# The up product of an MLP as seven block products for groups two to four, with sums of the rows beside group one

## The chip, the core and the metric

The kernel runs on one core of a Trainium2 chip. The core has TensorE (PE in the profile) for matrix products, VectorE (DVE) and ScalarE (ACT) for element-wise work, GpSimd (POOL) and SyncE (SP), which here mainly issue transfers, and 16 DMA engines that the issued transfers share. A product accumulates in a bank of PSUM of 128 x 512 numbers. The metric is the device time of one execution, in microseconds; shorter is better.

## The reference

A layer of 512 tokens with 1024 features: a projection, two recurrent branches, a gated mix and its output projection, and then an MLP of 4096 features. All of it is in float32. The change touches the MLP, and the transfers that are made earlier on its behalf:

```python
    mix = (jax.nn.sigmoid(gate_a) * ya + jax.nn.sigmoid(gate_b) * yb) @ w_out
    x = x + rmsnorm(mix, n_mix_post)
    hn = rmsnorm(x, n_mlp_pre)
    ff = jnp.square(jax.nn.relu(hn @ w_up)) @ w_down
    return x + rmsnorm(ff, n_mlp_post)
```

## The kernel before

**Products of split numbers.** A float32 operand is held as a high part, rounded to the shorter float32r, and a low part, the rest. Every product is three matmuls: high by high, high by low, low by high (the helper `mm3`, L93 to L95; L317 in the block products). A weight tile of 128 x 1024 comes as `raw` by a load on SP's queue (L103 from the weights, L197 from block sums); ACT rounds it to `whi` (L148) and DVE subtracts to get `wlo` (L149). There are two `raw` buffers per pool and three of `whi` and `wlo`. One such tile feeds 24 matmuls of 512 columns.

**The MLP.** The 4096 features are done in four groups of 1024. A group is an up product, the squared relu, and a down product that adds into `facc`, four row tiles of 128 tokens. In the up product the features are the output's partitions and the 512 tokens its columns: 64 products of 128 x 128 weights by 512 tokens, 192 matmuls. Group one alone begins while the rows of the residual stream are still being normalised: `mix_done` adds a row tile's norm to `x2`, scales the row (`fw`, L1763), and PE transposes it to `hn` (L397), whose cast is on ACT (L428) and whose low part is on DVE (L429). So group one's first four output tiles take the second 256 tokens first and the first 256 after them, as matmuls of 256 columns.

**Seven products for eight.** The down product of a group is a block product of a 2 x 2 scheme by quarters: rows by a feature half and a token half, weights by a feature half and a column half. Seven products of quarter sums replace eight of quarters: "11", "12", "22" take plain quarters of the rows, "s1" to "s4" take sums. Row sums are made on DVE in `first_sums` (L1828 to L1830) and `other_sums` (L1838), and each is split (L1786: cast on ACT, subtraction on DVE). Weight sums are made by transfers alone (`BlockSums`): a copy of a quarter to DRAM on SP's queue (L169), then an accumulating add on POOL's queue (L135), both of 512 KB. The products of a sum write two banks, `dl` or `mm`, and DVE adds them to `facc` (L1851).

**When the block sums are made.** The copies and adds wait in two lists. `pace` is called at each weight load; when the modelled PE time has passed `queued[0]`, it issues one job behind that load and moves `queued[0]` on by `JOB_US` (8.5), and over the stretch `REST` (860 to 985) in one step. A job that is late is not made up except by one at each following load; a sum that is wanted and not made is made on the spot.

**Order.** A scheduler orders each engine's instructions by data, buffers and priority; after that, each engine runs its own list strictly in order. `high_priority` moves instructions ahead: the weight splits and the first sums are so marked. The two finished row tiles of tokens 0 to 255 (`early`) are stored from `x2` to the output by SP in group three, and the MLP's result is later added to them in DRAM.

## Time and profile before

Three executions took 1328.65, 1331.12 and 1333.48 us, median 1331.12. The execution that was profiled spans 1329.4 us, 1.7 below that median.

| | of the profiled execution |
|---|---|
| span | 1329.4 us |
| PE busy | 1314.3 us, 99% |
| DVE busy | 938.0 us, 71% |
| ACT busy | 663.9 us, 50% |
| POOL busy | 89.6 us, 7% |
| moved by DMA | 223.16 MB, mean 168 GB/s |
| groups two to four, up | 43.52 us each |
| groups two to four, down | 38.08 us each |

A row of instructions gives line, engine, operation, output and inputs by the program's names, shape, count, then the busy time and the mean of one. A row of a window gives the stretch, its length, and each engine's busy time with its instructions, then the clock that PE was granted (1.00 is full speed), the busy share of the DMA engines and the GB/s that they moved. A row of a timeline gives an instruction's start, its duration and, in brackets, the idle time ahead of it with what ended it. Instructions overlap at their ends, so a start-to-start distance is shorter than a duration.

### The profile page before, as it was taken

The page shows a single profiled execution, that of the slowest core. Times are in us where ns is not written, and L with a number is a line of the kernel's source. Part 1 is how long each engine was busy: PE and PEld are TensorE (multiplying, and loading weights), DVE is VectorE, ACT ScalarE, POOL GpSimd, SP SyncE. Part 2 cuts the span into 40 slices and gives each one's busy share as a digit, 9 for nine tenths or more (in the row PEclk, how much of TensorE's full clock was granted, in tenths as well). Part 3 has the DMA queues.
Part 4 walks back from the last instruction along what each step waited for, and adds up shares of the span by engine and source line. Part 5 has one row for each costly group of instructions (what it writes and reads, how often), then busy time and mean ns, then how long its engine had stood idle before and what let it go on. Part 6 is the DMA issues. An engine that isn't in the chain of part 4 may idle for free.

```text
span 1329.4 us, 17531 instructions
## 1 busy us (share of the span) xinstructions
PE 1314.3 (99%) x6591; PEld 1093.6 (82%) x6591; DVE 938.0 (71%) x1569; ACT 663.9 (50%) x1159; POOL 89.6 (7%) x95
## 2 busy tenths in 40 slices
PE   9999999999999999999999999999999999999997
PEld 7888888888788888888888888888889888888886
DVE  6889867586656577877577766889675746738378
ACT  5784335555524533554453353455356636355364
POOL 2201100000010000000010000000001000000001
PEclk9999999999999999999999999999999999999999
DMA  6336944467765665986393472445629896868635
GB/s 191 133 112 159 203 101 94 110 164 194 188 159 151 143 187 142 270 244 155 95 259 89 104 229 80 141 150 173 233 78 248 225 275 147 234 187 225 188 118 135
DMA packets 115558, 223.16 MB, mean 168 GB/s; under 512 B 6983, under 2 KB 38897, under 8 KB 114961
## 3 DMA queue, kind: packets, MB, share of 16 engines
q1 hardware_dynamic: 96496, 175.13, 41.2%
q0 software_dynamic: 16944, 40.54, 18.9%
q10 hardware_dynamic: 2032, 6.36, 1.3%
q8 instruction: 52, 0.85, 0.2%
q14 instruction: 34, 0.27, 0.1%
HBM read 216.75 MB, written 72.37 MB: 217 GB/s over the span
## 4 chain that ended last, share of the span: by engine, by line
PE 89%; DVE 4%; ACT 4%; DMA 2%; issue 1%; DVEq 0%; ACTq 0%
PE mm L668 18%; PE mm L317 16%; PE dl L317 11%; PE mm L95 10%; PE mm L93 10%; PE mm L94 10%; PE dl L668 6%; DMA raw<-sums 1%; PE dl L93 1%; PE tr L397 1%; PE dl L95 1%; PE dl L94 1%; PE tr L677 1%; DVE wlo L149 1%; PE mm L632 1%
## 5 line engine op out<-in xcount | busy, mean ns | idle before, releaser
L149 DVE TENSOR_TENSOR wlo<-raw,whi 128x1024 fp32r<-128x1024 f32 x269 | 328.5, 1223 | 215.7 <-ACT whi L148 214.3
L148 ACT CAST whi<-raw 128x1024 fp32r<-128x1024 f32 x269 | 282.7, 1052 | 376.4 <-PE mm L668 74.6
L668 PE MATMUL mm<-actT,whi 128*128 128x512 f32 x448 | 144.8, 404 | 0.0
L317 PE MATMUL mm<-whi,xsum 128*128 128x512 f32 x384 | 120.6, 390 | 0.0
L95 PE MATMUL mm<-hn,wlo 128*128 128x512 f32 (+1 forms) x288 | 105.4, 366 | 0.0
L94 PE MATMUL mm<-hn,whi 128*128 128x512 f32 (+1 forms) x288 | 105.3, 366 | 0.0
L93 PE MATMUL mm<-hn,whi 128*128 128x512 f32 (+1 forms) x288 | 105.3, 366 | 0.0
L668 PEld LDWEIGHTS mm<-actT,whi 128*128 128x128 f32 x448 | 81.7, 190 | 15.3
L668 PE MATMUL mm<-actT,wlo 128*128 128x512 f32 x224 | 88.4, 395 | 0.0
L317 PEld LDWEIGHTS mm<-whi,xsum 128*128 128x128 f32 x384 | 71.8, 188 | 14.9
L317 PE MATMUL mm<-wlo,xsum 128*128 128x512 f32 x192 | 74.8, 390 | 0.0
L317 PE MATMUL dl<-whi,ffq 128*128 128x512 f32 x224 | 71.2, 389 | 0.0
L668 PE MATMUL mm<-whi,og 128*128 128x512 f32 x192 | 62.4, 397 | 0.0
L95 PEld LDWEIGHTS mm<-hn,wlo 128*128 128x128 f32 x288 | 54.3, 189 | 8.8
L94 PEld LDWEIGHTS mm<-hn,whi 128*128 128x128 f32 x288 | 54.3, 189 | 8.8
L93 PEld LDWEIGHTS mm<-hn,whi 128*128 128x128 f32 x288 | 54.3, 189 | 8.6
L668 PE MATMUL mm<-whi,actT 128*128 128x512 f32 x176 | 60.3, 405 | 1.0 <-DVE qf L906 1.0
L317 PE MATMUL dl<-whi,actT 128*128 128x512 f32 x192 | 61.2, 390 | 0.0
L317 PE MATMUL mm<-whi,ffq 128*128 128x512 f32 x192 | 60.9, 389 | 0.0
L1786 DVE TENSOR_TENSOR ffq<-r,ffq 128x512 fp32r<-128x512 f32 (+1 forms) x64 | 39.2, 622 | 27.8 <-ACT ffq L1786 27.6
L135 POOL DMA_DIRECT2D sums<-in_w_in_dram x28 | 32.6, 1164 | 364.3 <-DMA sums<-in_w_in_dram 364.3
L93 PE MATMUL mm<-actT,whi 128*128 128x512 f32 x128 | 51.5, 402 | 0.0
(391 smaller groups left out, 2843.0 us busy)
## 6 DMA issues: line engine op xcount, KB each, us to landing
raw<-in_w_in_dram SPq DMA_DIRECT2D x95, 512.0 KB, 4.6
raw<-sums SPq DMA_DIRECT2D x64, 512.0 KB, 4.5
raw<-in_w_up_dram SPq DMA_DIRECT2D x36, 512.0 KB, 7.1
sums<-in_w_in_dram SPq DMA_DIRECT2D x32, 512.0 KB, 5.6
sums<-in_w_down_dram SPq DMA_DIRECT2D x32, 512.0 KB, 7.4
sums<-in_w_in_dram POOLq DMA_DIRECT2D x28, 512.0 KB, 7.5
raw<-in_w_down_dram SPq DMA_DIRECT2D x24, 512.0 KB, 4.2
sums<-sums POOLq DMA_DIRECT2D x20, 512.0 KB, 8.4
```

Of the source, the lines that this page charges most:

```text
L93: nc.tensor.matmul(ps, lh, rh, start=first, stop=False)
L94: nc.tensor.matmul(ps, lh, rl, start=False, stop=False)
L95: nc.tensor.matmul(ps, ll, rh, start=False, stop=last)
L135: tc.keep_in_program_order(nc.gpsimd.dma_start(dst, src, accum_op=ALU.add))
L148: nc.scalar.copy(hi[:, :n], raw[:, :n])
L149: nc.vector.tensor_tensor(lo[:, :n], raw[:, :n], hi[:, :n], ALU.subtract)
L317: m = nc.tensor.matmul(pss[t], lhs[i // 2], rhs[i % 2], start=first and k + i == 0, stop=k + i == 5, skip_group_check=not first,)
L397: nc.tensor.transpose(ps, src, ident)
L632: pin(nc.tensor.matmul(first_keys[f][:, 256:512], ws[w][:, kk, :], xs[x][:, 2 * j + kk, 256:512], start=False, stop=kk == 1 and i == 2, sk ...
L668: m = tc.keep_in_program_order(nc.tensor.matmul(*args, **kwargs))
L677: tc.keep_in_program_order(nc.tensor.transpose(ps, src, ident if by is None else by))
L1786: return nc.scalar.copy(dst[0], r), nc.vector.tensor_tensor(dst[1], r, dst[0], ALU.subtract)
```

## The change

The up product of groups two to four becomes a block product of the same seven-product scheme (`seven_up`). Its row operand is quarters of `hn` and four sums of quarters; its weight operand is quarters of `w_up` and four block sums of them for each of the three groups, which doubles the lists of transfers for the MLP's last three groups: 24 copies and 24 adds more. Each of the seven products is 48 matmuls of 256 columns: 336 matmuls for 192 of 512. It takes 14 weight splits for 8. The seven results are combined by `combine` on DVE, and `Squares.square` applies the squared relu to a whole quarter (forms of 128 x 1024 where there were 128 x 512).

`hidden_sums` makes the four row sums: eight additions or subtractions of 128 x 1024 on DVE, then four casts on ACT and four low parts on DVE. They are written behind group one in the code. Their scratch is `facc`, which moves to the place that `x2` had; `x2` gets tiles of its own, and one of these is the place of a sum once the early rows are stored, a store that moves from SP in group three to POOL ahead of the sums.

`JOB_US` becomes 4.6, except between 480 and 640, where it stays 8.5. In `seven_down` the product "12" stands later in the order of groups two to four: in groups two and three behind "s2" and "s1", in group four still directly behind "11".

```diff
-JOBS_FROM, JOB_US = 70.0, 8.5
+JOBS_FROM, JOB_US, BUSY_JOB_US = 70.0, 4.6, 8.5
+BUSY = 480.0, 640.0
...
-        queued[0] += JOB_US
+        queued[0] += BUSY_JOB_US if BUSY[0] < queued[0] < BUSY[1] else JOB_US
...
-    down_sums = [BlockSums(w_down[grp * D : (grp + 1) * D, :], 0, 512, f"dn{grp}") for grp in range(4)]
-    for sums in [z_sums, ga_sums] + vg_sums + [gb_sums] + down_sums:
+    down_sums, up_sums = [], {}
+    for grp in range(4):
+        if grp:
+            up_sums[grp] = BlockSums(w_up, grp * D, grp * D + 512, f"up{grp}")
+        down_sums.append(BlockSums(w_down[grp * D : (grp + 1) * D, :], 0, 512, f"dn{grp}"))
+    mlp_sums = [sums for grp in range(4) for sums in (up_sums.get(grp), down_sums[grp]) if sums]
+    for sums in [z_sums, ga_sums] + vg_sums + [gb_sums] + mlp_sums:
...
-        x2 = acc.rearrange("p k t -> p (k t)").rearrange("p (t d) -> p t d", t=4)
+        x2 = Rows2([pm.tile([P, 2, D], F32, tag=f"x2{i}", name="x2") for i in range(2)])
...
+            def square(self, th, ch, src):
+
+                r = self.quarter(th, ch)
+                for i in range(2):
+                    nc.scalar.activation(r[:, 2 * i : 2 * i + 2, :], src[i], AF.Relu)
+                nc.scalar.activation(r, r, AF.Square)
+                name = {(0, 0): "11", (0, 1): "12", (1, 1): "22"}.get((th, ch))
+                if name:
+                    split(r, self.dst[name])
+
+            def first_sums(self, f, n=2):
+
+                fs = slice(f, f + n)
                 r11, r21, r22 = self.r[:, 0, 0, fs, :], self.r[:, 0, 1, fs, :], self.r[:, 1, 1, fs, :]
                 nc.vector.tensor_tensor(r22, r21, r22, ALU.subtract)
                 nc.vector.tensor_tensor(r21, r11, r21, ALU.subtract)
                 nc.vector.tensor_tensor(r11, r22, r11, ALU.subtract)
-                self.sums_mark = split(r11, self.fs("s2", f))[0]
-
-            def other_sums(self, f, last):
-
-                r, fs = self.r[:, :, :, f : f + 2, :], lambda name: self.fs(name, f)
+                self.sums_mark = split(r11, self.fs("s2", f, n))[0]
...
-            b = bank(psm)
-            plain(b, "12", 1, 0, True)
-            add(0, 0, b, prio=0)
+            def late():
+                b = bank(psm)
+                plain(b, "12", 1, 0, True)
+                add(0, 0, b, prio=0)
+
+            if not grp:
+                late()
             c = bank(psm)
 
             def s1():
...
                 summed(a, "s3", 3, False)
                 add(1, 1, a, ALU.subtract)
 
-            for step in (s1, s2) if grp == 3 else (s2, s1, s3):
+            for step in (late, s1, s2) if grp == 3 else (s2, s1, late, s3) if grp else (s2, s1, s3):
...
-        facc = pm.tile([P, 4, D], F32, tag="facc", name="facc")
+        facc = cp.tile([P, 4, D], F32, tag="acc", name="facc")
+        hq = {"11": quarter(hn, 0, 0), "12": quarter(hn, 1, 0), "22": quarter(hn, 1, 1)}
+
+        def hidden_sums():
+
+            for t in early:
+                nc.gpsimd.dma_start(out[0, t * P : (t + 1) * P, :], x2[:, t, :])
+
+            def by_features(w):
+                return w.rearrange("p (k t) -> p k t", k=4)
+
+            def pair(name):
+                return [by_features(pm.tile([P, D], F32R, tag="ym", name=name, bufs=4)) for _ in range(2)]
+
+            s1 = pm.tile([P, 2, 4, 256], F32R, tag="x20", name="hsum")
+            places = {
+                0: [s1[:, i] for i in range(2)],
+                1: pair("hsum"),
+                2: pair("hsum"),
+                3: quarter(hn, 0, 1),
+            }
+            a22, a11 = by_features(facc[:, 0, :]), by_features(facc[:, 1, :])
+            a21 = by_features(facc[:, 2, :])
+            a12 = by_features(facc[:, 3, :])
+            sum_quarters(hn, ((a22, a11), a21, a12), lambda i: places[i], hq)
+
+        def seven_up(grp, sq):
+
+            src, c1, sums = w_up, grp * D, up_sums[grp]
+            pinned = []
+
+            def product(pss, x, ks, wts, first):
+                wh, wl = wts
+                xh, xl = hq[x]
+                for f in range(4):
+                    for kk in range(2):
+                        k = 2 * ks + kk
+                        w = [v[:, kk, f * P : (f + 1) * P] for v in (wh, wl)]
+                        tick(768)
+                        for i in range(3):
+                            m = nc.tensor.matmul(
+                                pss[f // 2][:, f % 2 * 256 : f % 2 * 256 + 256], w[i // 2], (xh, xl)[i % 2][:, k, :],
+                                start=first and f % 2 + k + i == 0, stop=k + i == 5, skip_group_check=True,
+                            )
+                            if pinned:
+                                tc.keep_in_program_order(m)
+                            pinned.append(m)
+
+            plain, summed = block_products(src, sums, product)
+
+            def halves_of(th, ch):
+                q = sq.quarter(th, ch).rearrange("p f t -> p (f t)")
+                return [q[:, 512 * i : 512 * i + 512] for i in range(2)]
+
+            def take(th, ch, parts):
+                sq.square(th, ch, [p.rearrange("p (f t) -> p f t", f=2) for p in parts])
+
+            def combine(dst, ps, other, op):
+                with tc.high_priority(400):
+                    for i in range(2):
+                        nc.vector.tensor_tensor(dst[i], ps[i], other[i], op)
+
+            p1, u2 = halves_of(1, 0), halves_of(0, 1)
+            a = bank(psx)
+            plain(a, "11", 0, c1, True)
+            with tc.high_priority(400):
+                for i in range(2):
+                    nc.scalar.copy(p1[i], a[i])
+            b = bank(psm)
+            summed(b, "s2", 2, True)
+            combine(u2, b, p1, ALU.add)
+            plain(a, "12", 1, c1, False)
+            take(0, 0, a)
+            summed(b, "s3", 3, False)
+            combine(p1, b, p1, ALU.add)
+            c = bank(psm)
+            summed(c, "s1", 1, True)
+            combine(halves_of(1, 1), c, p1, ALU.subtract)
+            take(1, 1, halves_of(1, 1))
+            d = bank(psx)
+            summed(d, "22", 4, True)
+            with tc.high_priority(150):
+                combine(p1, d, p1, ALU.add)
+                take(1, 0, p1)
+                sq.first_sums(0, 4)
+            plain(c, "s4", 1, c1 + 512, False)
+            combine(u2, c, u2, ALU.subtract)
+            take(0, 1, u2)
+            sq.other_sums(0, grp == 3, 4)
+
         for grp in range(4):
             sq = Squares(grp)
-            for th in (None,) if grp else (1, 0):
-                tt = slice(0, T) if th is None else slice(256 * th, 256 * th + 256)
+            if grp:
+                seven_up(grp, sq)
+                seven_down(grp, sq.dst)
+                continue
+            for th in (1, 0):
+                tt = slice(256 * th, 256 * th + 256)
                 pss = feature_major(w_up, [h[:, :, tt] for h in hn], grp * 1024, 512, 8)
                 for f in range(4):
                     sq.take(0, f, pss[f], th)
...
                     for i in range(2):
                         sq.take(1, f + i, pss[i])
                     sq.first_sums(f)
-                sq.other_sums(f, grp == 3)
-            if grp == 2:
-                for t in early:
-                    with tc.issue_after(sq.sums_mark.ins):
-                        nc.sync.dma_start(out[0, t * P : (t + 1) * P, :], x2[:, t, :])
+                sq.other_sums(f, False)
+            hidden_sums()
             seven_down(grp, sq.dst)
```

The lines of the changed kernel are shifted by a few: its L104 is L103 before, L136 is L135, L150 is L149, L170 is L169, L198 is L197, L435 is L429, L1745 is L1738, L1770 is L1763, L1793 is L1786, L1848 to L1850 are L1828 to L1830, L1858 is L1838, L1871 is L1851. L223 to L231 are `sum_quarters`, L1976 the store of the early rows, L2030 `combine`.

**First place: DVE in group one, from the second-to-last row tile's norm to the last row's transposes** (`acc` or `x` is the residual row, `hn` here the low part of the transposed row). Before:

```order
L416 SCALAR_TENSOR_TENSOR nr_y<-nr_t,nr_y 128x1
L1738 SCALAR_TENSOR_TENSOR acc<-fw,nr_y,acc 128x512
L429 TENSOR_TENSOR hn<-tr,hn 128x4x128
L149 TENSOR_TENSOR wlo<-raw,whi 128x1024
L429 TENSOR_TENSOR hn<-tr,hn 128x4x128
L1738 SCALAR_TENSOR_TENSOR acc<-fw,nr_y,acc 128x512
L1723 TENSOR_SCALAR nh_v<-nh_s 128x1
L149 TENSOR_TENSOR wlo<-raw,whi 128x1024
```

and, a few rows on:

```order
L1763 SCALAR_TENSOR_TENSOR fw<-acc,nr_y,wmlp 128x512 x2
L149 TENSOR_TENSOR wlo<-raw,whi 128x1024
L429 TENSOR_TENSOR hn<-tr,hn 128x4x128 x2
L149 TENSOR_TENSOR wlo<-raw,whi 128x1024 x4
L1786 TENSOR_TENSOR ffq<-r_8593,ffq 128x256 x2
```

Now:

```order
L1730 TENSOR_SCALAR nh_v<-nh_s 128x1
L223 TENSOR_TENSOR facc<-hn 128x1024
L421 TENSOR_TENSOR nr_t<-nr_t,nh_v 128x1
L1731 SCALAR_TENSOR_TENSOR nh_v<-nh_s,nh_v 128x1
L224 TENSOR_TENSOR facc<-facc 128x1024
L150 TENSOR_TENSOR wlo<-raw,whi 128x1024
L422 SCALAR_TENSOR_TENSOR nr_y<-nr_t,nr_y 128x1
L418 RECIPROCAL nr_y<-nr_y 128x1
L1770 SCALAR_TENSOR_TENSOR fw<-x_8205,nr_y,wmlp 128x512 x2
L150 TENSOR_TENSOR wlo<-raw,whi 128x1024
L435 TENSOR_TENSOR hn<-tr,hn 128x4x128 x2
```

and, at the last row:

```order
L422 SCALAR_TENSOR_TENSOR nr_y<-nr_t,nr_y 128x1
L1770 SCALAR_TENSOR_TENSOR fw<-x_8205,nr_y,wmlp 128x512 x2
L231 TENSOR_TENSOR hsum<-facc,hsum 128x1024
L435 TENSOR_TENSOR hn<-tr,hn 128x4x128 x2
L223 TENSOR_TENSOR facc<-hn 128x1024 x2
L225 TENSOR_TENSOR facc<-facc 128x1024
```

From the end of the third row's norm to the last row's `fw`, three sums of 128 x 1024 (another L223 stands eight rows ahead of the first of these) are now in DVE's list, and seven weight splits instead of five; between that `fw` and the low part of `hn` stands the low part of a row sum. On PE, 205 matmuls of group one's up product stand behind the last row's transposes before, 192 now.

**Second place: DVE where group four's up product hands over to its down product** (`r` is the squared rows, `ffq` the low part of a row operand, `dl` and `mm` banks of PSUM). Before:

```order
L1786 TENSOR_TENSOR ffq<-r_10500,ffq 128x2x256
L149 TENSOR_TENSOR wlo<-raw,whi 128x1024
L1786 TENSOR_TENSOR ffq<-r_10500,ffq 128x2x256
L1828 TENSOR_TENSOR r_10500<-r_10500 128x512
L149 TENSOR_TENSOR wlo<-raw,whi 128x1024
L1829 TENSOR_TENSOR r_10500<-r_10500 128x512
L1851 TENSOR_TENSOR facc<-facc,dl 128x512
L1830 TENSOR_TENSOR r_10500<-r_10500 128x512
```

Now:

```order
L2030 TENSOR_TENSOR r_10923<-dl,r_10923 128x512 x2
L1793 TENSOR_TENSOR ffq<-r_10923,ffq 128x1024
L150 TENSOR_TENSOR wlo<-raw,whi 128x1024
L1848 TENSOR_TENSOR r_10923<-r_10923 128x1024
L150 TENSOR_TENSOR wlo<-raw,whi 128x1024
L2030 TENSOR_TENSOR r_10923<-mm,r_10923 128x512 x2
L1849 TENSOR_TENSOR r_10923<-r_10923 128x1024
L150 TENSOR_TENSOR wlo<-raw,whi 128x1024
L1850 TENSOR_TENSOR r_10923<-r_10923 128x1024
L150 TENSOR_TENSOR wlo<-raw,whi 128x1024
L1871 TENSOR_TENSOR facc<-facc,dl 128x512
L1793 TENSOR_TENSOR ffq<-r_10923,ffq 128x1024
```

followed by `L150`, the second `L1871`, and then two `L1793`, the first of which is the low part of "12". Where two 128 x 512 sums stood between splits, whole quarters now stand: the rows of the first sums are 128 x 1024, and the last quarter's `combine` waits for the last up product. In groups two and three the list reads the same as far as the second `L1871`, except that what is wanted there first is the low part of "s2", the `L1793` ahead of that `L150`.

**Third place: SP's queue at the output projection** (`w_br_b`, `w_out`, `w_up` are loads of weights, `sums<-` are copies for the block sums). Before:

```order
L197 DMA raw<-in_w_in_dram 128x2x512 x2
L103 DMA raw<-in_w_br_b_dram 128x1024 x4
L103 DMA raw<-in_w_out_dram 128x1024 x8
L103 DMA raw<-in_w_up_dram 128x2x512 x4
L1964 DMA out_dram<-acc 128x1024
L103 DMA raw<-in_w_up_dram 128x2x512 x4
```

Now:

```order
L104 DMA raw<-in_w_br_b_dram 128x1024 x2
L170 DMA sums<-in_w_up_dram 128x2x512
L104 DMA raw<-in_w_br_b_dram 128x1024 x2
L170 DMA sums<-in_w_up_dram 128x2x512
L104 DMA raw<-in_w_out_dram 128x1024 x2
L170 DMA sums<-in_w_up_dram 128x2x512
L104 DMA raw<-in_w_out_dram 128x1024 x2
L170 DMA sums<-in_w_up_dram 128x2x512
L104 DMA raw<-in_w_out_dram 128x1024 x2
L170 DMA sums<-in_w_down_dram 128x2x512
L104 DMA raw<-in_w_out_dram 128x1024 x2
L170 DMA sums<-in_w_down_dram 128x2x512
```

Where no job stood among the last loads ahead of the MLP, a copy now stands behind every second one.

21 lines of the change are left out of this document (12 added, 9 removed).

## The prediction

> **What bounds the kernel now.** I began with the page: busy times and the chain of waits.
>
> ```profile
> span 1329.4 us, 17531 instructions
> PE 1314.3 (99%) x6591; PEld 1093.6 (82%) x6591; DVE 938.0 (71%) x1569; ACT 663.9 (50%) x1159; POOL 89.6 (7%) x95
> PE 89%; DVE 4%; ACT 4%; DMA 2%; issue 1%; DVEq 0%; ACTq 0%
> ```
>
> PE is the bound: only fewer matmul microseconds or fewer gaps shorten this kernel. Next the windows of group two's up and down product and of group four's up product (columns: stretch, length, busy time of PE, its weight loads, DVE, ACT, POOL, then clock, DMA share, GB/s):
>
> ```profile
> 1076.47:1119.99 43.52, 43.52 (x193) 36.04 (x192) 17.87 (x23) 22.26 (x35) 3.12 (x3) 1.00 0.73 188
> 1119.99:1158.07 38.08, 38.08 (x169) 31.53 (x168) 30.17 (x37) 18.88 (x21) 1.99 (x2) 1.00 0.79 232
> 1239.67:1283.19 43.52, 43.52 (x193) 36.04 (x192) 20.02 (x26) 21.79 (x34) 0.00 (x0) 1.00 0.39 120
> ```
>
> PE has no gap in the MLP: 192 matmuls of 512 columns take 43.52 us, 0.2267 each, and 168 take 38.08 at the same pace. So every gap that the change opens is new, and the saving is exact. DVE is half idle here on the mean; what matters is its order where PE waits for it.
>
> **The matmuls.** The price of 256 columns is in group one's timeline on PE:
>
> ```profile
> 999.05 0.28 PE L93 MATMUL mm<-hn,whi 128*128 128x256 f32 x1
> ...
> 1001.69 0.28 PE L94 MATMUL mm<-hn,whi 128*128 128x256 f32 x1
> 1001.81 0.28 PE L95 MATMUL mm<-hn,wlo 128*128 128x256 f32 x1
> 1002.39 0.63 PE L397 MATMUL tr<-cmat,fw 128*128 128x128 f32 x4 [0.30 <-DVE fw L1763]
> ```
>
> From 999.05 to 1001.69 stand 22 intervals: 0.120 us each, not half of 0.2267. Three groups save 3 x (43.52 - 336 x 0.120) = 3 x 3.20 = **9.6 us**, and not the 3 x 5.4 that an eighth of the columns would be. With each matmul loading its own weights in the rows behind 0.120 as in the new product, I hold that to within 0.3 per group.
>
> **Durations on DVE and ACT.** The new work has forms that the trace shows (groups by form in the MLP's part of the trace; the last number ahead of the second bar is the mean of one in ns):
>
> ```profile
> L149 DVE TENSOR_TENSOR wlo<-raw,whi 128x1024 fp32r<-128x1024 f32 x108 | 131.9, 1222 | 96.0 <-ACT whi L148 95.8
> L148 ACT CAST whi<-raw 128x1024 fp32r<-128x1024 f32 x108 | 113.5, 1053 | 131.1 <-PE mm L94 50.1 <-PE mm L317 26.1 <-PE dl L317 20.8
> L1781 ACT ACTIVATE r<-mm 128x512 f32<-128x512 f32 x28 | 16.6, 592 | 13.8 <-PE mm L95 13.8
> L1851 DVE TENSOR_TENSOR facc<-facc,dl 128x512 f32<-128x512 f32 x22 | 14.5, 680 | 0.0
> L257 DVE TENSOR_TENSOR raw<-raw 128x1024 f32<-128x1024 f32 x4 | 4.9, 1221 | 0.1
> ```
>
> One follows the next sooner than its duration. DVE's timeline at group two's hand-over:
>
> ```profile
> 1115.31 0.68 DVE L1786 TENSOR_TENSOR ffq<-r,ffq 128x512 fp32r<-128x512 f32 x1
> 1115.91 1.22 DVE L149 TENSOR_TENSOR wlo<-raw,whi 128x1024 fp32r<-128x1024 f32 x1
> 1117.04 0.68 DVE L1786 TENSOR_TENSOR ffq<-r,ffq 128x512 fp32r<-128x512 f32 x1
> ```
>
> So DVE's pace is 1.13 us for 128 x 1024 (1115.91 to 1117.04) and 0.60 for 128 x 512 (1115.31 to 1115.91).
>
> **Group one: +6.** PE reaches the last row's transposes just as DVE finishes `fw`; the row at 1002.39 shows 0.30 us of idle time. DVE around it:
>
> ```profile
> 1001.49 1.42 DVE L1763 SCALAR_TENSOR_TENSOR fw<-acc,nr_y,wmlp 128x512 f32<-128x512 f32 x2
> 1002.82 1.22 DVE L149 TENSOR_TENSOR wlo<-raw,whi 128x1024 fp32r<-128x1024 f32 x1
> 1003.96 1.28 DVE L429 TENSOR_TENSOR hn<-tr,hn 128x512 fp32r<-128x512 f32 x2
> ```
>
> There is no slack. Ahead of that `fw` the order now has three row sums and two splits more: 5 x 1.13 = 5.7 us. Against that, 205 matmuls stood behind the last transposes before and 192 do now: 13 x 0.12 = 1.6 us of PE work goes ahead and covers part. Net 4.1. Then the low part of a row sum stands ahead of `hn`'s low part on DVE (1.13), and its cast ahead of `hn`'s on ACT (1.05 by the 1053 ns row): about 2 more, since PE has nothing between the transposes and the first matmul on `hn`. Together 6. From below it is 0, if the sums fall into DVE's idle time (0.27 us stood ahead of the reciprocal here, so there is little of it). From above it is 9: the cast's target is the place of the early rows, free only when POOL has stored them, and POOL's queue has block-sum adds ahead of that store. I take 6, from the order of rows.
>
> **Hand-over in groups two and three: +2.4 each.** Let D be the end of the up product "22". The up product "s4" (48 x 0.12 = 5.8) and the down product "11" (24 x 0.2267 = 5.4) follow, so "s2" is wanted at D + 11.2. It writes the `dl` banks that hold "11", so DVE must have added them to `facc`, and it needs the low part of "s2". DVE's list from D: one `combine` (0.6; the first half's bank is complete earlier), low part of "22" 1.13, split 1.13, first sum 1.13, split 1.13, two `combine` 1.2, second sum 1.13, split, third sum, split (3.4): 10.9 and some 0.4 of waits for ACT, then the add of the first bank to D + 11.9, low part of "s2" to 13.0, split 1.13, add of the second bank to 14.7. PE's first six matmuls (1.36) start near 12 but the third waits for the low part; the next six wait for the second bank, D + 14.95 where 12.56 was wanted: 2.4. From below 0, if the scheduler's order leaves ACT and DVE ahead of this walk; from above 4.
>
> **Group four: +4.5.** There "12" follows "11" directly, and is wanted at D + 11.2, its low part 0.45 later. By the order that low part is behind the same list, behind "s2"'s low part, a split and the second add: 14.7 + 1.13 = 15.9, and 0.25 to start, against 11.65. From below 0, from above 6 with the tail's last splits a little late.
>
> All other added DVE work lies beside matmuls: the remaining row sums once, and for each group six more splits and ten `combine` rows, 6 x 1.13 + 10 x 0.60 = 12.8 us on a DVE that was busy 17.87 of 43.52 and 30.17 of 38.08. Outside the hand-overs I cost it at nothing; the matmuls hide it, and without that cover it would be the 12.8.
>
> **Transfers: +3.** 48 jobs more, and from 70 to 480 and 640 to 860 at 4.6 us for 8.5:
>
> ```profile
> q1 hardware_dynamic: 96496, 175.13, 41.2%
> q0 software_dynamic: 16944, 40.54, 18.9%
> ...
> raw<-in_w_in_dram SPq DMA_DIRECT2D x95, 512.0 KB, 4.6
> raw<-in_w_up_dram SPq DMA_DIRECT2D x36, 512.0 KB, 7.1
> ...
> raw<-in_w_out_dram SPq DMA_DIRECT2D x8, 512.0 KB, 4.2
> ```
>
> ```profile
> 300.00:400.00 100.00, 99.11 (x452) 81.93 (x451) 61.42 (x95) 46.66 (x80) 7.95 (x7) 1.00 0.70 180
> 500.00:600.00 100.00, 100.00 (x448) 82.81 (x447) 81.87 (x108) 47.12 (x63) 6.55 (x6) 1.00 0.80 220
> 1000.00:1100.00 100.00, 99.70 (x505) 85.20 (x504) 55.53 (x70) 57.28 (x89) 11.99 (x12) 1.00 0.93 249
> ```
>
> POOL's queue q0 took 18.9% of 1329.4 = 251 us, about 3.9 for each of the 64 adds; q1's 548 us over the page's 290 or so SP issues are 1.9. A job is then about 2.9 us of all engines, a share of 0.34 at one in 8.5 us and 0.63 at one in 4.6: the stretch at 0.70 goes to about 0.99. The row at 0.93 has PE busy 99.70 of 100, so a full queue alone is no stall. From below 0. From above 12: the eight `w_out` loads get copies among them; at the busy time's 7.1 us for a load instead of 4.2, and two buffers, (7.1 - 4.2) / 2 = 1.5 each, all eight exposed. I take a quarter of that, since the row at 0.93 is the nearest to the new state.
>
> **Sum.** -9.6 + 6 + 2 x 2.4 + 4.5 + 3 = +8.7. On the profiled 1329.4 this is 1338.1; that execution is 1.7 below the median of 1331.12, so **1340 us**.
>
> **Rivals.**
>
> *The bubbles are hidden.* Then only the matmuls count: 1331.1 - 9.6 = 1321.5. For it: DVE's mean share, and splits that the scheduler might place earlier than their data. Against it: an engine runs its list in order, and the 0.30 us row shows no slack in group one. Faster by over 0.3% (below 1327.1; that is about what a measurement of this kernel tells from no change) needs stalls under 5.6 of my 18.3. Chance 0.12.
>
> *Stalls and saving balance.* Half the group-one term and no term for transfers: 1331.1 - 9.6 + 3 + 4.8 + 4.5 = 1333.8. Chance 0.23 for the band 1327.1 to 1335.1.
>
> *Transfers decide.* In 300 to 400, ACT already waited for loads:
>
> ```profile
> ACT whi L148 <- DMA raw<-sums: 12.2, 5, 3.7
> ACT whi L148 <- DMA raw<-in_w_in_dram: 8.3, 3, 6.2
> ```
>
> If at a share near 1 each load comes late by as much as `w_up` against `w_in` (7.1 - 4.6 = 2.5 us), two buffers hide about half, and with one load in four exposed that way over 600 us (some 130 loads) it is 130 / 4 x 1.25 = 40 us at worst; with the row at 0.93 against it I price the case at 15 instead of 3: 1352. It decides once loads wait in PE's path outside the MLP. Chance 0.12, slower.
>
> *The clock drops behind the two long bubbles.* The trace has a stretch in which PE's clock was halved (same columns as above):
>
> ```profile
> 161.00:164.00 3.00, 3.00 (x9) 2.23 (x7) 2.76 (x5) 0.63 (x1) 0.00 (x0) 0.51 1.06 220
> 164.00:167.00 3.00, 3.00 (x36) 2.42 (x35) 1.13 (x2) 0.00 (x0) 0.00 (x0) 0.92 0.98 186
> ```
>
> It lost 3 x 0.49 + 3 x 0.08 = 1.7 us. With one such stretch behind each gap of over 4 us (group one, group four) the time is 1339.8 + 3.4 = 1343. Against it: no gap of that length stands in the MLP before, so nothing here shows the point from which it happens. Chance 0.08, slower. The Trainium skill, "TensorE: Matmul & The Clock Gate", section "HAM oscillation — how this bites in real kernels", says that PE falls to half clock when it idles for a window of more than about 3.4 us; by that rule both gaps, 4.4 and 4.5 us, are long enough, and whether they fill a window depends on its phase.
>
> **How the numbers follow.** My own walk, 1340 within 1335 to 1346, has 0.45; with the two slower rivals 0.65 for slower by over 0.3%, 0.23 for within, 0.12 for faster. The range 1328 to 1352 goes up to the case of transfers and down into the balance, leaving out the hidden bubbles and the worst of the transfers.
>
> **What would show it.** Up windows of groups two to four of 40.3 us with PE full: the saving. An idle time on PE of about 4 us ahead of the last transposes, released by `fw`, then 1 to 2 us released by ACT and DVE: group one. Idle time released by DVE's adds to `facc` and by `ffq` early in the down windows, which become 40.5 us (groups two and three) and 42.6 or more (group four). Windows before 980 us that hold as many matmuls as before would make the transfers' term 0; idle time on PE there behind `whi`, released by DMA, would raise it. I am wrong in sign if the gaps on PE in the MLP sum to under 9.6.

## The result

The changed kernel takes 1376.1 us (median of four, 1372.98 to 1382.02), the kernel before 1330.1 (median of four): a ratio of 1.0347, 95% interval 1.0322 to 1.0371. Slower was forecast, but by 9 us; it is 46, and outside the range. The page of the changed kernel, against the lines shown of before:

```profile
span 1379.9 us, 18566 instructions
PE 1323.7 (96%) x7023; PEld 1113.2 (81%) x7023; DVE 985.1 (71%) x1590; ACT 679.3 (49%) x1148; POOL 116.4 (8%) x121
q1 hardware_dynamic: 101488, 196.11, 44.6%
q0 software_dynamic: 22224, 54.17, 23.6%
PE 71%; DMA 11%; DVE 9%; ACT 6%; issue 2%; SPq 0%; DVEq 0%; ACTq 0%
raw<-in_w_in_dram SPq DMA_DIRECT2D x95, 512.0 KB, 6.7
```

PE is still busiest, but 15.1 us of its span were idle before and 56.2 are now; DMA stands on the chain that ended last with 11% instead of 2%, and a load of `w_in` lands in 6.7 us instead of 4.6. Windows by stage say where. Before, the stretch ahead of the MLP's first up matmul and group one's up product:

```profile
0.00:990.98 990.98, 984.24 (x5039) 816.67 (x5040) 724.93 (x1272) 482.56 (x889) 64.32 (x69) 1.00 0.58 157
990.98:1038.39 47.41, 47.04 (x305) 42.84 (x304) 31.26 (x56) 29.90 (x58) 7.77 (x8) 1.00 1.00 258
```

After, the same two, then group one's down product, group two's up and down, group three's, and group four's:

```profile
0.00:1028.89 1028.89, 996.07 (x5040) 820.62 (x5040) 724.80 (x1272) 481.14 (x889) 97.68 (x101) 0.99 0.70 183
1028.89:1083.62 54.73, 49.72 (x306) 45.09 (x305) 43.69 (x67) 33.36 (x62) 9.24 (x10) 0.94 0.91 234
1083.62:1124.52 40.90, 38.63 (x169) 31.46 (x168) 25.58 (x31) 22.45 (x28) 4.81 (x5) 1.00 1.01 267
1124.52:1165.71 41.19, 40.58 (x338) 40.37 (x337) 26.05 (x27) 24.91 (x29) 1.13 (x1) 1.00 0.75 225
1165.71:1206.31 40.60, 38.97 (x171) 31.31 (x169) 34.18 (x37) 20.45 (x21) 0.00 (x0) 1.00 0.59 183
1206.31:1246.62 40.31, 40.31 (x337) 40.31 (x336) 26.43 (x28) 24.86 (x28) 0.00 (x0) 1.00 0.60 182
...
1287.19:1327.51 40.32, 40.32 (x338) 40.31 (x337) 26.44 (x28) 24.85 (x28) 0.00 (x0) 1.00 0.60 183
1327.51:1371.92 44.41, 40.20 (x170) 32.42 (x168) 39.12 (x61) 25.84 (x40) 3.57 (x4) 0.96 0.45 125
```

| stage | before | after | difference | forecast |
|---|---|---|---|---|
| ahead of the MLP's first up matmul | 990.98 | 1028.89 | +37.9 | +3 (all transfers) |
| group one, up | 47.41 | 54.73 | +7.3 | +6 |
| group one, down | 38.08 | 40.90 | +2.8 | 0 |
| up, groups two to four | 130.56 | 121.82 | -8.7 | -9.6 |
| down, groups two and three | 76.16 | 81.17 | +5.0 | +4.8 |
| down, group four | 38.24 | 44.41 | +6.2 | +4.5 |
| sum, the profiled execution | | | +50.5 | +8.7 |

(Group three's down product, left out above, is 1246.62 to 1287.19, 40.57. The profiled execution took 1382.0 us, 5.9 above the median, so its differences sum to more than 46; its span is some 2 us shorter than its time, as in every run here.) In the MLP most stages came out near the walk; group one's down product, which had no term, and group four's are the exceptions. The 5039 or 5040 matmuls ahead of the MLP are the same, and they took 38 us longer: PE was idle there for 32.8 us instead of 6.7, and busy for 11.8 us more with the same matmuls, most of it at a lower clock, as a later section shows.

Matmul for matmul (worked out from the starts of the n-th matmul in both traces, in the time of the kernel before), 5.5 us were lost between 300 and 350, 14.2 between 550 and 600, 6.6 between 750 and 800 and 8.6 between 860 and 900. The jobs, the copies and adds for the block sums, explain the places better than the interval does:

| us of the trace | 70 to 300 | 300 to 480 | 480 to 640 | 640 to 860 | 860 to 990 |
|---|---|---|---|---|---|
| jobs issued before | 31 | 22 | 21 | 19 | 0 |
| jobs issued after | 33 | 32 | 32 | 37 | 18 |
| weight loads after | 29 | 31 | 32 | 38 | 29 |

Between 480 and 640, where the interval was to stay at 8.5, there was a job for every load, as elsewhere up to 860, and there most was lost. By the code, a job is issued only at a load, and the loads come some 5 to 6 us apart. `queued[0]` gains 4.6 per job and so falls behind: after the 65 jobs issued by 480 us it stands near 70 + 65 x 4.6 = 369 (an estimate from these counts). Until it has caught up, every load issues a job, whatever the interval is. The stretch without jobs from 860 on was missed in the same way.

What PE waited for is in the view of its waits in the changed kernel (total, times, longest):

```profile
PE dl L94 <- ACT osq L1579: 7.7, 2, 4.2
PE tr L403 <- DVE fw L1770: 4.7, 1, 4.7
PE dl L323 <- ACT whi L149: 4.6, 3, 1.6
PE mm L323 <- DVE ffq L1793: 4.2, 1, 4.2
PE mm L323 <- DVE wlo L150: 3.2, 4, 1.3
PE mm L323 <- ACT whi L149: 2.6, 1, 2.6
PE dl L323 <- DVE facc L1871: 2.6, 4, 0.8
PE dl L323 <- DVE wlo L150: 2.3, 3, 0.8
PE dl L674 <- ACT vt L1336: 2.1, 1, 2.1
PE dl L674 <- DVE st L1331: 2.0, 1, 2.0
```

The second row is group one's stall (4.4 by the walk), the fourth group four's (4.5 by it), the row on `facc` with two short waits on `ffq` the hand-overs. All but 3 us of the rest lies ahead of the MLP, 30 us there from 70 us on, and names engines, not transfers. Of these 30, 12 are waits for a weight's `whi` or `wlo`, so for a late load at one remove; nine of them stand between 555 and 600 us, in the place of the greatest loss. The longest one there, and a window behind it in which PE ran at half clock (0.50):

```profile
572.56 0.50 PE L323 MATMUL mm<-whi,xsum 128*128 128x512 f32 x1 [2.59 <-ACT whi L149]
```

```profile
575.00:576.00 1.00, 1.00 (x4) 0.81 (x3) 1.00 (x2) 0.87 (x2) 0.73 (x1) 0.50 1.07 287
```

For the other waits the engines had waited first. In ACT's and DVE's timelines around one of those waits, the 2.0 us on `st`:

```profile
333.03 1.05 ACT L149 CAST whi<-raw 128x1024 fp32r<-128x1024 f32 x1 [2.26 <-DMA raw<-sums]
```

```profile
334.11 1.23 DVE L150 TENSOR_TENSOR wlo<-raw,whi 128x1024 fp32r<-128x1024 f32 x1 [4.03 <-ACT whi L149]
335.25 0.68 DVE L1331 COPY st<-dl 128x512 f32<-128x512 f32 x1
```

A load came late; ACT stood at its cast, DVE behind it at the subtraction; and the copy that PE's recurrence wanted stood behind that in DVE's list, though it has nothing to do with the load. In this way a late load stops PE although PE waits for no weight. That the loads themselves were held back for a sum that was not made yet is ruled out: the waits of SP's queue between 70 and 1029 us name no add.

### The profile page after: what moved, and what is told of

Same layout as the page of the kernel before. It is cut to its first block, busy times and chain, and to the rows that moved or that the text cites. A ratio compares the mean times of both kernels' runs of the same rounds, so it can differ in the third digit from the quotient of the medians.

```text
span 1379.9 us, 18566 instructions
## 1 busy us (share of the span) xinstructions
PE 1323.7 (96%) x7023; PEld 1113.2 (81%) x7023; DVE 985.1 (71%) x1590; ACT 679.3 (49%) x1148; POOL 116.4 (8%) x121
## 4 chain that ended last, share of the span: by engine, by line
PE 71%; DMA 11%; DVE 9%; ACT 6%; issue 2%; SPq 0%; DVEq 0%; ACTq 0%
PE mm L674 16%; PE mm L323 11%; PE dl L323 7%; DMA raw<-sums 6%; PE mm L95 6%; PE mm L96 6%; PE mm L94 6%; PE dl L674 5%; PE mm L2010 4%; PE dl L2010 3%; DVE wlo L150 3%; DMA raw<-in_w_in_dram 3%; ACT whi L149 2%; PE tr L683 1%; PE tr L403 1%
## 5 line engine op out<-in xcount | busy, mean ns | idle before, releaser
L150 DVE TENSOR_TENSOR wlo<-raw,whi 128x1024 fp32r<-128x1024 f32 x287 | 350.3, 1222 | 233.4 <-ACT whi L149 232.4
L149 ACT CAST whi<-raw 128x1024 fp32r<-128x1024 f32 x287 | 301.0, 1050 | 422.2 <-PE mm L674 76.6
L674 PE MATMUL mm<-actT,whi 128*128 128x512 f32 x448 | 143.7, 402 | 0.0
L674 PEld LDWEIGHTS mm<-actT,whi 128*128 128x128 f32 x448 | 81.1, 188 | 15.1
L674 PE MATMUL mm<-actT,wlo 128*128 128x512 f32 x224 | 87.7, 391 | 0.0
L136 POOL DMA_DIRECT2D sums<-sums x32 | 26.8, 837 | 473.7 <-DMA sums<-in_w_down_dram 184.0
L136 POOL DMA_DIRECT2D sums<-in_w_in_dram x28 | 32.6, 1192 | 282.5 <-DMA sums<-in_w_in_dram 282.5
L323 PEld LDWEIGHTS dl<-whi,ffq 128*128 128x128 f32 x224 | 41.9, 188 | 16.1 <-ACT ffq L1793 2.3
L94 PE MATMUL mm<-actT,whi 128*128 128x512 f32 x128 | 52.5, 410 | 0.0
L2010 PE MATMUL dl<-hn,whi 128*128 128x256 f32 x288 | 52.2, 283 | 0.0
L2010 PE MATMUL mm<-hsum,whi 128*128 128x256 f32 x288 | 52.1, 283 | 0.0
L95 PE MATMUL mm<-actT,whi 128*128 128x512 f32 x128 | 51.6, 403 | 0.0
L96 PE MATMUL mm<-actT,wlo 128*128 128x512 f32 x128 | 51.5, 403 | 0.0
L674 PEld LDWEIGHTS mm<-actT,wlo 128*128 128x128 f32 x224 | 42.0, 188 | 9.3
```

The lines of the kernel that those rows point to most:

```text
L94: nc.tensor.matmul(ps, lh, rh, start=first, stop=False)
L95: nc.tensor.matmul(ps, lh, rl, start=False, stop=False)
L96: nc.tensor.matmul(ps, ll, rh, start=False, stop=last)
L136: tc.keep_in_program_order(nc.gpsimd.dma_start(dst, src, accum_op=ALU.add))
L149: nc.scalar.copy(hi[:, :n], raw[:, :n])
L150: nc.vector.tensor_tensor(lo[:, :n], raw[:, :n], hi[:, :n], ALU.subtract)
```

## The experiments

**Pace of the jobs, and the MLP by itself.** First the interval alone in the kernel before:

```diff
-JOBS_FROM, JOB_US = 70.0, 8.5
+JOBS_FROM, JOB_US, BUSY_JOB_US = 70.0, 4.6, 8.5
+BUSY = 480.0, 640.0
...
-        queued[0] += JOB_US
+        queued[0] += BUSY_JOB_US if BUSY[0] < queued[0] < BUSY[1] else JOB_US
```

> The kernel before with one edit: the interval of jobs is 4.6 us except in 480 to 640. The MLP, and the number of jobs (128), stay as before. In the changed kernel's trace the stretch up to the first up matmul of the MLP takes 1028.9 us instead of 991.0. Theory A (the crowding of transfers ahead of the MLP costs the 38 us, whatever the transfers are for): most of it comes back here, 1355 to 1368. Theory B (it is the number of jobs, or what the MLP's new products do, not their pace): within 5 us of before, 1327 to 1337.

1357.8 us, ratio 1.0196 (1.0168 to 1.0224). Its row for the stretch ahead of the MLP:

```profile
0.00:1021.86 1021.86, 997.43 (x5040) 822.77 (x5040) 724.90 (x1272) 480.70 (x889) 85.79 (x90) 0.99 0.65 170
```

30.9 of the 37.9 us, with no other part of the change and the MLP untouched (both profiled executions are some us above their medians; by the medians the whole loss is 26.1 of 46). Of 128 jobs, 124 were issued by 800 us instead of 91. Up to 640 us the jobs are those of the changed kernel (96 for 97); between 860 and 990 there is none, and nothing is lost there. This is what theory A said. Then the MLP without its new sums:

```diff
-JOBS_FROM, JOB_US, BUSY_JOB_US = 70.0, 4.6, 8.5
+JOBS_FROM, JOB_US, BUSY_JOB_US = 70.0, 8.5, 8.5
...
-            up_sums[grp] = BlockSums(w_up, grp * D, grp * D + 512, f"up{grp}")
+            up_sums[grp] = None
...
+            class sums:
+                def weights(i, ks):
+                    kh, c = ((0, c1 + 512), (0, c1), (1, c1 + 512), (1, c1))[i - 1]
+                    return weights(src, 4 * kh + 2 * ks, 2, c, 512, paced=False)
```

> The changed kernel with the interval of before (8.5 us) and without the block sums of w_up: where a product wants a sum it loads a plain quarter of w_up instead, so the sums of the weights are left out and the same number of loads, splits and matmuls is there. 128 jobs as before. Theory A: the MLP alone remains: -8.7 us for three up products, +7.3 for group one, +2.5 twice, and +6.2 in group four, as the changed kernel's trace shows them, without the +2.8 of group one's down product: 1330.1 + 9.8 = 1340, between 1335 and 1344. Theory B: it stays near the changed kernel, over 1360.

1345.1, ratio 1.0101 (1.0078 to 1.0123), just above the range of theory A: 4 us of the excess stand in group four's up product, 44.3 us instead of 40.3, where ACT's timeline shows 5.1 us of idling for a load of `w_up` among late jobs. The two parts, 26 and 13, make 39 of the 46.

The interval of before with all the new jobs:

```diff
-JOBS_FROM, JOB_US, BUSY_JOB_US = 70.0, 4.6, 8.5
+JOBS_FROM, JOB_US, BUSY_JOB_US = 70.0, 8.5, 8.5
```

> The changed kernel with one edit: the interval is 8.5 us everywhere. All 176 jobs remain, and what is not made in time is made at its use, in the MLP. Theory A (pace): the stretch ahead of the MLP is back to within 5 us of 991, and part of the loss returns in the MLP, where the late jobs crowd: 1340 to 1365. Theory B (number of jobs): no better than the changed kernel, 1370 or more.

1430.6, ratio 1.0742 (1.0717 to 1.0768). The time is in theory B's range, but not for its reason: ahead of the MLP it is back at 989.8, as theory A said, and what was late cost far more than A allowed. Group three's up and down product:

```profile
1165.20:1225.80 60.60, 44.57 (x338) 43.58 (x337) 25.68 (x27) 24.29 (x28) 8.04 (x8) 0.86 0.83 222
1225.80:1288.14 62.34, 43.53 (x170) 34.15 (x169) 33.50 (x36) 20.64 (x22) 7.35 (x8) 0.84 0.85 207
```

60.6 and 62.3 for 40.3 and 40.6. A sum that is made at its use is a chain of a copy, an add and a load with nothing under it; PE waited 7.5 and 7.6 us for the cast of a weight in that up product, and 13.5 for an addition to `facc` in the down product. So the short interval was not chosen without need: at 8.5 the new sums come too late, and at 4.6 the loads ahead of the MLP do.

**Which transfers, and why.** The first edit was to tell whether copies in front of loads on SP's queue are the trouble, and could not tell:

```diff
-            nc.sync.dma_start(self.t[i][:, k : k + 2, :], self.first[i][:, k : k + 2, :])
+            nc.scalar.dma_start(self.t[i][:, k : k + 2, :], self.first[i][:, k : k + 2, :])
```

> The changed kernel with one edit: the copies are issued on ACT's queue instead of SP's. Theory A1 (the loads wait because the engines and the memory are shared): no gain, within 8 us of the changed kernel's 1376. Theory A2 (the loads wait because the copies stand ahead of them in the same queue): 15 us or more of the 38 come back, 1361 or less.

1471.0, ratio 1.1046 (1.1022 to 1.1071), which neither theory had. On ACT's list the scheduler did not keep the copies behind the loads that pace them: 71 of the 88 were issued by 300 us (17 in the changed kernel), and the time ahead of the MLP went to 1118.5. It says nothing about the queue. The next one does:

```diff
-        tc.keep_in_program_order(nc.gpsimd.dma_start(dst, src, accum_op=ALU.add))
```

> The kernel before with the interval of 4.6 us (8.5 in 480 to 640) and with all accumulating adds left out, so that the block sums are only copies of their first block; the 64 copies stay at their places among the loads. The kernel with that interval and all jobs took 1357.8, 26 above the kernel before. Theory A1 (loads share engines and memory with the jobs, and an add, which reads two blocks and writes one, is the dearer job): the loss ahead of the MLP is gone, 1326 to 1334. Theory A2 (it is the copies ahead of the loads in SP's queue): most of the loss stays, 1345 or more.

1331.3, ratio 1.0008 (0.9995 to 1.0021). Its row for the stretch ahead of the MLP:

```profile
0.00:992.04 992.04, 986.49 (x5040) 819.13 (x5040) 725.85 (x1272) 482.30 (x889) 18.29 (x26) 1.00 0.43 141
```

With the copies at the same places in SP's list and only the adds gone, the whole loss is gone, as A1 said. That leaves what makes an add dear:

```diff
-        tc.keep_in_program_order(nc.gpsimd.dma_start(dst, src, accum_op=ALU.add))
+        tc.keep_in_program_order(nc.gpsimd.dma_start(dst, src))
```

> The kernel before with the interval of 4.6 us (8.5 in 480 to 640), in which every accumulating add is a plain transfer from the same source to the same destination on the same queue, so that the sums are left out and only the last block stays. With the adds it took 1357.8, without them 1331.3. If an add is dear because it is one transfer more behind which loads wait: most of the 26 us stay, 1345 to 1358. If it is dear because it accumulates (it also reads the destination, or is handled more slowly): 1331 to 1340.

1340.7, ratio 1.0098 (1.0075 to 1.0120); the result is between the two answers, at the edge of the second. With adds the loss was 26.1, with plain transfers in their place 11.3: somewhat more than half of the price is the accumulation. The queue rows of the two pages, the kernel with adds and then the one with plain transfers:

```profile
q0 software_dynamic: 16944, 40.54, 18.4%
sums<-in_w_in_dram POOLq DMA_DIRECT2D x28, 512.0 KB, 7.4
```

```profile
q0 software_dynamic: 11312, 40.54, 10.2%
sums<-in_w_in_dram POOLq DMA_DIRECT2D x28, 512.0 KB, 4.8
```

The same 40.54 MB are booked, but the accumulating form takes 16944 packets instead of 11312 and 18.4% of the engines' time instead of 10.2%. The loads show the rest. For 144 of the 164 weight loads issued between 70 and 990 us before, and 141 of 159 after, the trace has the landing. These are the medians from the end of the issue to the landing by what was in flight then (worked out from the landing times of the trace, leaving out transfers without a known landing and those within 0.3 us of it; in brackets the number of loads):

| no other load in flight, and | kernel before | changed kernel |
|---|---|---|
| nothing else | 3.5 (57) | 3.4 (37) |
| one copy | 4.8 (5) | 3.7 (5) |
| one add | 5.2 (16) | 6.1 (16) |
| one copy and one add | 9.0 (3) | 8.2 (4) |
| two adds | none | 10.1 (4) |

One add makes a load half again as slow or more; an add with a copy, or two adds, make it more than twice as slow, up to three times. One copy alone does less (4.8 and 3.7 us; the groups of three to five loads are small). In the changed kernel 37 of these loads met nothing else in flight instead of 57. By the waits ahead of the MLP, ACT stood for loads of `w_in` 20.5 us in 8 waits before and 60.1 in 21 waits after:

```profile
ACT whi L148 <- DMA raw<-in_w_in_dram: 20.5, 8, 6.2
```

```profile
ACT whi L149 <- DMA raw<-in_w_in_dram: 60.1, 21, 7.1
```

The Trainium skill, "DMA: Bandwidth & Descriptors", section "Queues, rings and completion order", says that each DMA engine takes turns between the queues it has work for, packet by packet. The rows agree in so far as a load on SP's queue is slower beside an add on POOL's (5.2 to 6.1 us for 3.4 to 3.5), which stands in another queue; that the turns go packet by packet no row here shows.

**The changed kernel without adds, and the MLP's terms.** The same line is taken out of the changed kernel:

```diff
-        tc.keep_in_program_order(nc.gpsimd.dma_start(dst, src, accum_op=ALU.add))
```

> The changed kernel with all accumulating adds left out (the block sums are only copies of their first block); 88 copies, loads, matmuls and the work of DVE and ACT stay. Theory (the adds are the whole price of the transfers): the stretch ahead of the MLP's first up matmul is within 2 us of the 991.0 of before instead of 1028.9, and only the MLP's own terms remain, -9.6 for the matmuls, +7 to 8.5 for group one, 2 x 2.5 and +6 to 7: 1338 to 1343. Rival (the copies and the new order cost too): over 1350.

1341.0, ratio 1.0073 (1.0058 to 1.0088). The stretch ahead of the MLP:

```profile
0.00:992.22 992.22, 986.32 (x5040) 818.85 (x5040) 725.13 (x1272) 482.38 (x889) 18.70 (x27) 1.00 0.46 151
```

It is 992.2 for the 991.0 of before, so the 88 copies cost little or nothing there. Group one's down product is back at 38.08. So the adds are 35 of the 46 us, and the MLP's own terms, 9.6, are nearly all the rest. Two edits then aim at the stalls of group one and group four, in the kernel without sums of `w_up`:

```diff
-            hidden_sums()
+            with tc.issue_after(last_lo[0].ins):
+                hidden_sums()
...
-            for step in (late, s1, s2) if grp == 3 else (s2, s1, late, s3) if grp else (s2, s1, s3):
+            for step in (s2, s1, late) if grp == 3 else (s2, s1, late, s3) if grp else (s2, s1, s3):
```

(`last_lo` is the instruction that writes the last row's low part of `hn`.)

> The kernel without block sums of w_up (8.5 us interval, sums of the weights left out, 1345.1) with two edits: the row sums are issued only after the last row's low part of hn, and group four's down product takes s2, s1, 12 in place of 12, s1, s2. My walk: the stall ahead of the last transposes goes (7 to 8 us with its slow clock), the 4.2 us ahead of 12 turn into the 1.6 of the other groups: 1331 to 1336. Rival: DVE is the bound behind both places, and the stalls move to the next product: 1340 or more.

1338.2, ratio 1.0055 (1.0034 to 1.0076). The two places did as said; the time is 2 us above the range, for a reason elsewhere. Group one's up product and group four's down product:

```profile
992.02:1039.41 47.39, 47.03 (x305) 42.83 (x304) 44.06 (x68) 33.48 (x62) 7.47 (x8) 1.00 0.95 242
1290.10:1330.84 40.74, 39.10 (x170) 31.13 (x168) 37.97 (x59) 26.09 (x40) 3.61 (x4) 1.00 0.44 129
```

Group one's 47.39 us is the 47.41 of before, although all row sums are still made. Against that, group four's up product took 49.4 us: PE waited 6.2 us at its start for an addition to `facc`, which stood in DVE's list behind splits of late loads, as in the run above.

Whether the clock is part of group one's term was tried in the same kernel without these edits:

```diff
+            if fill and not half:
+                with tc.issue_after(fill[0].ins):
+                    for _ in range(32):
+                        nc.tensor.matmul(
+                            ps.rearrange("p k t -> p (k t)")[:, 0:256], dst[0][:, 0, 256:384], dst[0][:, 0, 256:512],
+                            start=True, stop=True,
+                        )
```

(`fill` is set for the last row tile alone, `ps` is the bank of its transposes.)

> The kernel without block sums of w_up (1345.1) with 32 matmuls of 256 columns (3.8 us, results thrown away) put into PE's list of group one ahead of the last row's transposes, so that the stall of 4.7 us there shrinks below 1 us while the transposes start no sooner. Theory (PE's clock is halved behind a stall of that length): group one's up product, 55.0 us from its first matmul to its down product there, becomes about 2 us shorter, 53, with a clock of 1.00 in all of it. Rival (the slow clock has another cause, or the time is DVE's alone): it stays at 55 or grows by up to 3.8.

1342.3 us, ratio 1.0090 (1.0065 to 1.0114), for 1345.1. Group one's up product, without and with them:

```profile
990.01:1045.05 55.04, 49.93 (x306) 45.30 (x304) 43.67 (x67) 33.34 (x62) 7.48 (x8) 0.94 0.89 216
```

```profile
991.72:1042.58 50.86, 50.74 (x338) 46.70 (x336) 43.75 (x67) 33.60 (x62) 7.47 (x8) 1.00 0.91 230
```

32 matmuls more, and 4.2 us less in this stage (the intervals of the two whole times overlap). The clock is 1.00 where it was 0.94. It is twice what I expected, and not all of it need be the clock: the scheduler also left 206 matmuls behind the last transposes instead of 192, which puts 14 x 0.12 = 1.7 us more work behind them and less ahead. In the changed kernel the stall and what follows it stand on PE's timeline and in the windows behind it:

```profile
1046.10 1.94 PE L403 MATMUL tr<-cmat,fw 128*128 128x128 f32 x8 [4.67 <-DVE fw L1770]
```

```profile
1046.00:1049.00 3.00, 2.71 (x11) 2.34 (x12) 1.89 (x3) 2.02 (x3) 0.00 (x0) 0.50 0.99 138
1049.00:1052.00 3.00, 2.85 (x14) 2.56 (x13) 3.00 (x4) 0.00 (x0) 0.00 (x0) 0.50 0.76 190
1052.00:1055.00 3.00, 3.00 (x27) 3.00 (x27) 2.20 (x3) 1.05 (x1) 0.87 (x1) 0.98 0.42 67
```

4.67 us of idling, then six at half clock. The prediction's rival cites a rule of the Trainium skill, "TensorE: Matmul & The Clock Gate", section "HAM oscillation — how this bites in real kernels": half clock behind idling of more than about 3.4 us. It holds for this gap. It doesn't cover the shorter gaps of the last section, which half clock followed as well; there the measurement decides.

**An even interval, and the edits in the complete kernel.**

```diff
-JOBS_FROM, JOB_US, BUSY_JOB_US = 70.0, 4.6, 8.5
+JOBS_FROM, JOB_US, BUSY_JOB_US = 70.0, 6.4, 6.4
...
-REST = 860.0, 985.0
+REST = 2000.0, 2001.0
```

> The changed kernel with an interval of 6.4 us everywhere and no stretch without jobs. All 176 jobs; by the counts of the traces 144 to 160 must be issued by 1200 us, 176 by 1275. Theory (what counts is how many jobs stand among the same loads): between the two ends, about half of the 38 us ahead of the MLP (15 to 22 us) and few late jobs: 1350 to 1372. If the time were a matter of the number of jobs alone it would stay at 1376; if late jobs at their use decide, as with 8.5 us, over 1380.

1383.0, ratio 1.0390 (1.0368 to 1.0411), worse than the changed kernel, though the stretch ahead of the MLP fell to 1013.8, +23 for +38. This is no test of a thinner spacing: up to 640 us it issued 94 jobs for the changed kernel's 97, nearly one for each load again, and it had lost 23.3 us there for 22.7. The gain came behind that, with 43 jobs for 55. The time lies in the range given for late jobs, but not for that reason; group one took the gain back:

```profile
1013.78:1087.48 73.70, 50.60 (x305) 45.98 (x304) 41.27 (x63) 31.22 (x58) 13.42 (x14) 0.81 0.89 207
```

ACT's timeline shows the row sum's first cast at 1049.63, with 20.34 us of idling ahead of it. On POOL's queue the store of the second early row was issued at 1038.68, behind four adds, of which two had waited 10.4 and 8.1 us for other transfers; it landed at 1049.56, and only then was the cast's place free. PE waited 18.3 us for ACT there. This is the mechanism that the prediction had given as the upper bound of group one, 3 us there, 18.3 here.

The two edits from above and a third, here and in the next two kernels:

```diff
-                nc.gpsimd.dma_start(out[0, t * P : (t + 1) * P, :], x2[:, t, :])
+                nc.scalar.dma_start(out[0, t * P : (t + 1) * P, :], x2[:, t, :])
```

> The complete changed kernel with the three edits and an interval of 6.4 us everywhere with no stretch without jobs. With that interval alone it took 1383.0, with 73.7 us from group one's first up matmul to its down product, 18.3 of them in a wait of ACT for the early rows' place. By the terms group one returns to 47.4 and group four gains 3.9: 1383 - 26 - 4 = 1353, 1347 to 1360. If the loss there has another cause than the late store, over 1365.

1367.1, ratio 1.0272 (1.0255 to 1.0289). Group one is at 49.1, and its loss had the cause named; the time is 7 above the range, since late jobs now make group two's up product 44.4 us for 40.3 and its down product 42.3 for 40.6.

With the intervals of the changed kernel:

> The changed kernel, complete, with the three edits (row sums later, early rows stored by ACT's queue, group four s2, s1, 12) and its intervals of 4.6 and 8.5 us. By the terms 7.3 in group one and 3.9 in group four come back: 1376 - 11 = 1365, 1360 to 1370.

1364.6, ratio 1.0248 (1.0227 to 1.0268), as the terms gave it in sum, partly by luck: group one came to 49.1, so 5.6 of its 7.3 returned, and the stretch ahead of the MLP took 1021.6 in this profile for 1028.9.

And with the adds taken out as well:

> The same without adds, with three edits: the row sums are issued after the last row's low part of hn, the early rows are stored by ACT's queue instead of POOL's, and group four takes s2, s1, 12. By the terms: group one at the 47.4 us of before, three hand-overs at 2.5, three up products at 40.3: 1330.9 - 9.6 + 7.5 = 1329, 1326 to 1332. If the row sums collide with work behind them on DVE, 1334 or more.

1331.8, ratio 1.0002 (0.9993 to 1.0012): with the transfers' price and the two long stalls gone, no measurable difference from before. The 9.6 us of matmuls are used up by group one at 49.1 (+1.7, with 1.4 us of a wait on `fw` left) and three hand-overs of 2.5 each; 9.6 - 1.7 - 7.5 = 0.4.

```diff
-            take(1, 1, halves_of(1, 1))
+            with tc.high_priority(600):
+                take(1, 1, halves_of(1, 1))
```

> The changed kernel without adds and with the three edits (1331.8, the hand-overs at 40.6 to 40.7 us for 38.1), with one edit more: the squared relu of the quarter 22 is given priority 600, so that its low part stands ahead of the last quarter's combine. By rows of DVE's list s2's operand is then ready in time, but the split of 11's second tile comes behind the three sums, near D + 9.6 where D + 8.5 is wanted. If DVE's load is the bound of the hand-over, the wait moves from s2 to 11 and is 1.1 to 1.6 us: 1327 to 1330. If the order alone was at fault, all 2.5 go: 1324.

1331.2, ratio 1.0013 (1.0001 to 1.0026). The wait moved, as expected of a DVE that is full there, but it did not shrink to the 1.1 to 1.6 expected. PE in group two's hand-over:

```profile
1119.15 0.50 PE L322 MATMUL dl<-wlo,ffq 128*128 128x512 f32 x1 [0.82 <-DVE wlo L149]
...
1123.24 0.47 PE L322 MATMUL dl<-whi,ffq 128*128 128x512 f32 x1 [1.30 <-DVE facc L1871]
```

0.82 at the second tile of "11" and 1.30 at "s2", 2.1 together, and a window of 40.8 for 40.6. One change of order does not free the hand-over. Whether another does was not tried. None of the kernels run here beats the one before.

## Why the prediction was wrong

Its sign was right, and its size wrong by 37 us. By its own steps:

- *The matmuls, -9.6.* Right: 40.31 and 40.32 us for 40.32 forecast. In group two 41.19, with late weights.
- *Group one, +6.* The first part was right: the stall on `fw` was 4.67 for 4.4 forecast. The second was not: of the 2 us of waits for ACT and DVE behind the transposes, 0.20 came. In their place the clock that I kept for a rival came with the stall, six us at half clock, which is 3 us lost. That the term of 6 is near the 7.3 measured is in part luck.
- *Hand-over in groups two and three, +2.4 each.* 2.5 each, with the waits on `facc` and on the low part of "s2" that the walk named.
- *Group one's down product, no term.* It took 2.8 us more. PE's waits there are for a late weight, 1.5 us for `whi` and 0.8 for `wlo`, and without the adds it is back at 38.08; so it belongs to the transfers.
- *Group four, +4.5.* The wait was 4.21; the term 6.2, with the clock at 0.96 in that window.
- *Transfers, +3.* This is the step that failed. Its measured value is about 35: the changed kernel without adds is 35 us faster, and the pace alone costs the kernel before 26. The step took the share of busy DMA engines, worked out that it would go to 0.99 in 300 to 400 (it went to 0.88, since jobs can't come faster than loads), and then set it against the row at 0.93 with a full PE in the MLP. That row is no precedent. In 1000 to 1100 of the kernel before a load took 9.2 us in the median, and PE stayed full; in 300 to 400 of the changed kernel a load took 5.6, and PE lost 6.8 (from the landings that the traces have). So what a late load costs depends on what stands behind it. Two differences are known, and neither was tested by itself. In the MLP each load feeds work on DVE and ACT that waits for little else, while ahead of it chains of a recurrence share DVE's and ACT's lists with the splits. And in 300 to 400 there is one pool of two `raw` buffers, with at most one other load under way when a load was issued; in 1000 to 1100 the code has two pools, and up to three others were. The second can't be the whole of it, as up to three others were also under way between 550 and 600, where most was lost. The step also took the stretch from 480 to 640 as unchanged, and it had 32 jobs for 21. And the upper bound of 12 looked only at the eight loads of `w_out`, where 159 loads stood among the quicker jobs. The rival "transfers decide" named the place (300 to 400) and the rows, and its own arithmetic gave 40 us at worst. It was then priced down to 15 on the strength of the same row, and given 0.12.
- *The clock.* Its rival's mechanism was there in addition, and not instead: behind the long stalls of groups one and four, and ahead of the MLP too, at 575, 810 to 816 and 913 to 919 us (0.50). The mean granted clock fell from 0.997 to 0.988.

The stretch that the step spoke of, in the changed kernel:

```profile
300.00:400.00 100.00, 93.16 (x418) 75.32 (x417) 56.73 (x89) 41.98 (x73) 12.45 (x11) 1.00 0.88 213
```

PE is short of 6.8 us there at a share of 0.88, with 418 matmuls for 452, and with fewer GB/s than the 249 at which it was full in the MLP. The DMA share told me too little: it counts an engine as busy alike under a load and under an add, and what the loads felt was which job they met. The rows to use stood in the page of before: 3.9 us of all engines for an add against 1.9 for another transfer. I worked both out, and took their mean.

What stays open: the 11 us that plain transfers on POOL's queue cost, where copies on SP's queue cost nothing; and what the new sums would cost ahead of the MLP if the jobs were truly spaced out, which no run here did.

## What to carry to other kernels

Work that is moved to the DMA queues "in the background" has a price in the latency of the loads, and it is paid by whatever stands behind a load in an engine's list; so look at who waits behind the cast, not only at the share of the queues. Cost an accumulating transfer by its own row, and look at how often a load would meet one. If such work is paced by a clock, count in the trace whether it came at that pace. And before a product is traded for sums of its operands, walk the list of the engine that makes the sums at each hand-over: here 9.6 us of matmuls bought 9.2 of new waits even with the long stalls mended and the adds free.

## What was not expected of the hardware

- An accumulating DRAM transfer took 18.4% of the engines' time for 40.54 MB, a plain one on the same queue, with the same sizes, 10.2%; packets 16944 against 11312.
- Gaps on PE shorter than the one in group one were followed by half clock too. Behind 2.59 us of idling at 570 us, and one more of 0.76, PE ran at 0.50 to 0.67 from 574 until 578. Behind 1.59 and 0.76 us at 560 to 563 it ran at 0.50 from 564 to 567.
- Plain copies between DRAM tensors on SP's queue, at a short interval among the loads, cost no time that could be measured (ratio 1.0008, 0.9995 to 1.0021, without the adds).
